# A first stage with no arithmetic on GpSimd, side work paced by time, p and v panels in turn, and nine seven-product panels

## The chip, the cores and the metric

The kernel runs on one core of a Trainium2 chip. The metric is the device time of one execution in microseconds. Five engines share the work: TensorE (PE) multiplies, VectorE (DVE) and ScalarE (ACT) do elementwise work, GpSimd (POOL) does some arithmetic and issues the stores, SyncE (SP) issues the loads. Each engine takes its instructions strictly in the order in which the program emits them, as the rows of the trace show them; semaphores order the engines among each other.

## The reference, cut to what matters

One decoder layer for 1024 prompt tokens and 64 sample tokens (T = 1088 in all), width 1024:

```
mod = silu(c) @ w_mod + b_mod;  shift, scale, gate = split(mod, 3)
h = rmsnorm(x, norm_g) * (1 + scale) + shift
mg, u, va, za, q, k, vb, ob, zb, ig, fg, p, zc = split(h @ w_in)
ya = gelu(u) * spatial_gate(layernorm(gelu(va))) * silu(za)
yb = head_layernorm(sigmoid(ob) * mlstm(q, k, vb, ig, fg, state)) * silu(zb)
yc = (multiscale_pool(p) @ w_pool) * pool_scale * silu(zc)
merged = sum over the three branches of sigmoid(mg) * (y @ w_br)
y = rmsnorm(x + gate * (merged @ w_out))
```

`c` and so `scale` and `shift` differ between the prompt (one row) and the eight sample groups. New states of the mLSTM and of the pooling are outputs too.

## The kernel before, in words

**Products.** Every large product is made in fp32 accuracy from three reduced products: each operand is split into a high part (a cast on ACT) and a low part (a subtraction on DVE, `split`, L205), and PE adds high*high, high*low and low*high. The weights come in panels of 256 columns, each as four raw pieces of 128x512. The class `Stream` loads the pieces (`load`, SP), splits them (`step`: `whi` on ACT at L132, `wlo` on DVE at L101) and keeps at most eight split units.

**Panels.** `b_panel` (L258) makes features x tokens in six units of 24 matmuls of 362 to 364 columns. `a_panel` (L296) makes tokens x features in nine tiles. `seven` (L334) makes a b-panel's result by a seven-product scheme over halves of the inner dimension, of the tokens and of the features: 168 matmuls of 272 columns. It needs summed weights (DVE sums in `step`) and summed activations (`gen_factors`, L757, and `put_t4`, L794). The panels of `SEVEN` are made so: k, zb, zc, u, za and the first MG7 panels of mg; the other mg panels are b-panels in `merge_gates` (L1280).

**Stages.** `start` (L466) makes h and the panels q0 to q3; `seven_panels` (L799) follows; then `inputs_of_mixers` (L910) with `pool_branch` (L1183: p0, va0, p1, va1, ... and `gen_pool`), the panels v0 to v3 and ob0 to ob3; `merge_gates`; `finish` (L1718: the three branch products, then the output product).

**The first stage.** The order of the work is written out by hand in two strings, `PLAN_0` and `PLAN_1` (L1853). Each letter emits one small group of instructions on its engines, and no engine passes over an earlier letter. The letters: `1` loads a panel of w_mod (1 MB), `2` a tile of x (128 features x 1088 tokens, 0.56 MB), `3` a raw piece of w_in; `S` splits half a panel of w_mod; `M` multiplies it with silu(c) (16 matmuls); `C` copies the result out on ACT; `T` turns it on PE and makes two of the eight factors `am` = norm_g*(1+scale) (the first four panels) or shifts `sm` (the last four) on DVE; `Q` squares a tile of x on ACT and adds it to the sum `acc` on POOL (L581); `A`/`V` scale a tile by `am` on ACT or DVE; `H` makes its high part on ACT (L595), `L` its low part on DVE (L601); `W` splits one weight unit; `P`/`R` multiply a tile of x with panel q0 (first eight) or q1 (last eight), high and low parts; `e` makes the reciprocal roots (with a power on POOL); `f` spreads them over the tokens as `rb`; `v`/`g` multiply a tile by `rb` on DVE or POOL (L648); `m` adds the shift and splits the tile into `hhi`, `hlo` (ACT L656, DVE L658); `r` copies q0's or q1's sums out of PSUM; `z`, `s`, `t` make the share of the shift in q0 and q1; `w` keeps PE warm. So q0 and q1 are made from x times `am` before h is known, and `finish_rows` (L703) multiplies their rows by `rb` (on POOL) and adds the shift's share. All these tiles lie in 34 buffers (`slots`).

**After it.** q2 is a b-panel in the usual order, q3 one with all six units open at once (`kouter`), so that `put_t4` may write into h while q3 runs: the product with feature block k done, its factor may be made.

**Side work.** Python generators emit the rest of the work in small steps between the units and tiles of the panels. `tick` (L225) adds to `owed` and takes one step of the first generator per whole unit owed; `pace` sets what a unit or tile adds: 8.5 x pace per a-panel, 6 x pace per b-panel. pace is 1.2 in the pooling stage, 1.5 in v and ob, 1.4 later. The order of the generators: `gen_pool` behind each p panel; behind v0 `gen_gates` (gates of the mLSTM), `gen_sgu` (the spatial gate, three steps per tile of 128 tokens; its mixing product is L1029), `gen_gate` (the layer's gate), `gen_sample` and `gen_prompt` (the mLSTM). A `drain` in `finish` (branch 0, panel 3) ends what is left.

Of the kernel before, what the change touches and what calls it, by code (L numbers as in the profile page):

```python
# [11 lines left out]
ALU = mybir.AluOpType  # L12
# [20 lines left out]
MG7 = 5  # L33
PACE = 1.5
# [124 lines left out]
class Builder:  # L159
# [98 lines left out]
    def b_panel(self, panel, acts, evac, nk=KT, kouter=False, hook=None):  # L258
# [3 lines left out]
        units = [(f, g) for f in range(2) for g in range(3)]  # L262
# [22 lines left out]
        for u, (f, g) in enumerate(units):  # L285
# [7 lines left out]
            self.tick(self.pace / 2)  # L293
        self.st.used(panel)

    def a_panel(self, panel, acts, stack, evac, cols=256, order=range(9)):  # L296
# [4 lines left out]
        for u, t in enumerate(order):  # L301
            p = self.ps()
            if t < 8:
                ts = slice(t * 128, t * 128 + 128)
                for k in range(KT):
# [4 lines left out]
                    if k == 3:  # L310
                        self.tick(self.pace / 2)
# [11 lines left out]
            self.tick(self.pace / 2)  # L323
# [90 lines left out]
    def body(self):  # L414
# [7 lines left out]
        for nm_, ns in [(x, (n,)) for n in range(4) for x in ("p", "va")] + [(x, range(4)) for x in ("v", "ob")]:  # L422
# [43 lines left out]
    def start(self):  # L466
# [52 lines left out]
        A.copy(self.scs[:, :, 0:9], sc)  # L519
        V.tensor_tensor(out=self.scs[:, :, 32:41], in0=sc, in1=self.scs[:, :, 0:9].bitcast(F32), op=ALU.subtract)  # L520
# [9 lines left out]
        def mod_split():  # L530
            n, j = divmod(nxt("ms"), 2)
            raw = raws[n][j]
            hi = self.slot([128, 4, 256], F32R, name="ssh")
            lo = self.slot([128, 4, 256], F32R, name="ssl")
            m = 4 if n else 2
            for q in range(0, 4, m):
                self.split(*(x[:, q : q + m] for x in (raw, hi, lo)))
# [4 lines left out]
        def mod_mul():  # L542
# [3 lines left out]
            for kk in range(KT):  # L546
                for j in range(2):
                    PE.matmul(p[:64, :256], self.scs[:, kk, :], w[kk // 4][j][:, kk % 4, :],
                              start=(kk == 0 and j == 0), stop=(kk == KT - 1 and j == 1))
# [7 lines left out]
        def mod_turn():  # L557
# [3 lines left out]
            if n == 0:  # L561
                V.tensor_scalar(bmod[:, 1, :], bmod[:, 1, :], 1.0, None, ALU.add)
            for j in range(2):
                PE.matmul(p[:, j * 16 : j * 16 + 9], t[:, j * 128 : j * 128 + 128], sel, start=True, stop=True)
# [8 lines left out]
        def square():  # L573
# [4 lines left out]
            else:  # L578
                sq = self.slot([128, T], name="sq")
                A.activation(sq, xs[k], AF.Square)  # L580
                G.tensor_tensor(out=acc[0], in0=acc[0], in1=sq, op=ALU.add)  # L581

        def x_scale(on_act):
            k = nxt("xa")
            x = xs[k]
            V.tensor_tensor(out=bview(x[:, smp]), in0=bview(x[:, smp]), in1=bcol(am[:, k, 1:9]), op=ALU.mult)
            if on_act:
                A.activation(x[:, :TP], x[:, :TP], AF.Copy, scale=am[:, k, 0:1])
            else:
                V.tensor_scalar(x[:, :TP], x[:, :TP], am[:, k, 0:1], None, ALU.mult)  # L590

        def x_high():
            k = nxt("xh")
            hi = self.slot([128, T], F32R, name="xhi")
            A.copy(hi, xs[k])  # L595
# [1369 lines left out]
```

## Time and profile before

| what | value |
|---|---|
| runs, us | 1859.59, 1855.35, 1856.58 (median 1856.58) |
| the profiled execution, its own time | 1857.86 us |
| its span, first to last instruction | 1856.1 us |
| mean granted TensorE clock | 0.985 |
| first stage, to q2's first matmul | 119.31 us |
| q2 and q3 | 57.6 us |
| 25 seven-product panels | from 176.87 to 708.2 us |
| busy over the span: PE, DVE, ACT, POOL | 97%, 58%, 32%, 14% |

The span is the time from the first instruction to the last in the trace; 1.76 us of the execution's own time lie around it. A busy PE in these views is not a PE at its peak, since matmuls overlap; whether a stage runs at its best is seen by comparing its time with that of an undisturbed panel of the same kind.

### The profile page before, as it was taken

The page shows a single profiled execution, that of the slowest core. Times are in us where ns is not written, and L with a number is a line of the kernel's source. Part 1 is how long each engine was busy: PE and PEld are TensorE (multiplying, and loading weights), DVE is VectorE, ACT ScalarE, POOL GpSimd, SP SyncE. Part 2 cuts the span into 40 slices and gives each one's busy share as a digit, 9 for nine tenths or more (in the row PEclk, how much of TensorE's full clock was granted, in tenths as well). Part 3 has the DMA queues.
Part 4 walks back from the last instruction along what each step waited for, and adds up shares of the span by engine and source line. Part 5 has one row for each costly group of instructions (what it writes and reads, how often), then busy time and mean ns, then how long its engine had stood idle before and what let it go on. Part 6 is the DMA issues. An engine that isn't in the chain of part 4 may idle for free.

```text
span 1856.1 us, 32242 instructions
## 1 busy us (share of the span) xinstructions
PE 1796.1 (97%) x13017; PEld 1777.4 (96%) x13017; DVE 1071.9 (58%) x2003; ACT 586.0 (32%) x1141; POOL 262.3 (14%) x427
## 2 busy tenths in 40 slices
PE   7888999999999999999999999999999999999998
PEld 7888999999999998999999899999999999999998
DVE  7777556665666542434527955664655766564444
ACT  5443333333333332222223125332333231131224
POOL 3440000000000001110011212321101101200023
PEclk8988999999999999999999999999999999999999
DMA  6332323332222334333335754776457577694422
GB/s 252 108 128 74 106 94 94 104 122 80 71 70 76 130 106 150 121 123 101 94 116 189 217 180 125 240 237 201 143 175 231 179 228 208 184 317 142 151 62 97
DMA packets 142152, 270.42 MB, mean 146 GB/s; under 512 B 19377, under 2 KB 66161, under 8 KB 142003
## 3 DMA queue, kind: packets, MB, share of 16 engines
q1 hardware_dynamic: 118786, 184.20, 31.4%
q0 software_dynamic: 23072, 83.91, 13.3%
q8 instruction: 102, 1.67, 0.4%
q14 instruction: 48, 0.39, 0.1%
q10 hardware_dynamic: 144, 0.26, 0.0%
HBM read 179.96 MB, written 88.35 MB: 145 GB/s over the span
## 4 chain that ended last, share of the span: by engine, by line
PE 86%; DVE 8%; issue 2%; DMA 2%; ACT 1%; POOL 1%; SPq 0%; POOLq 0%; DVEq 0%; ACTq 0%
PE ps L270 30%; PE ps L308 15%; PE p L362 8%; PE y L362 8%; PE z L362 8%; PE x L362 4%; PE ps L614 2%; PE ps L316 1%; PE ps L1466 1%; PE ps L1264 1%; PE ps L1485 1%; PE ps L1682 1%; PE ps L1439 1%; PE ps L1468 1%; DMA ss<-in_w_mod_dram 1%
## 5 line engine op out<-in xcount | busy, mean ns | idle before, releaser
L101 DVE TENSOR_TENSOR wlo<-raw,whi 128x512 fp32r<-128x512 f32 (+1 forms) x272 | 189.7, 698 | 115.6 <-ACT whi L132 115.6
L308 PE MATMUL ps<-whi,hhi 128*128 128x256 f32 (+1 forms) x768 | 218.5, 284 | 0.0
L308 PE MATMUL ps<-wlo,hhi 128*128 128x256 f32 (+1 forms) x768 | 216.0, 281 | 0.0
L308 PE MATMUL ps<-whi,hlo 128*128 128x256 f32 (+1 forms) x768 | 215.1, 280 | 0.0
L270 PE MATMUL ps<-hhi,whi 128*128 128x362 f32 (+1 forms) x624 | 208.2, 334 | 5.5 <-DVE C L1494 3.4
L270 PE MATMUL ps<-hlo,whi 128*128 128x362 f32 (+1 forms) x624 | 207.0, 332 | 1.9 <-DMA hlo<-b12d 1.7
L270 PE MATMUL ps<-hhi,wlo 128*128 128x362 f32 (+1 forms) x624 | 206.6, 331 | 0.0
L270 PE MATMUL ps<-yhi,whi 128*128 128x362 f32 (+1 forms) x576 | 190.1, 330 | 3.0 <-DVE mgr L1742 1.6
L270 PE MATMUL ps<-yhi,wlo 128*128 128x362 f32 (+1 forms) x576 | 188.7, 328 | 0.0
L270 PE MATMUL ps<-ylo,whi 128*128 128x362 f32 (+1 forms) x576 | 188.5, 327 | 0.0
L132 ACT CAST whi<-raw 128x512 fp32r<-128x512 f32 (+1 forms) x272 | 162.3, 617 | 44.9 <-DVE raw L123 36.3
L308 PEld LDWEIGHTS ps<-whi,hhi 128*128 128x128 f32 x768 | 144.6, 188 | 0.8 <-issue 0.4
L308 PEld LDWEIGHTS ps<-wlo,hhi 128*128 128x128 f32 x768 | 144.7, 188 | 0.0
L308 PEld LDWEIGHTS ps<-whi,hlo 128*128 128x128 f32 x768 | 144.4, 188 | 0.0
L270 PEld LDWEIGHTS ps<-hhi,whi 128*128 128x128 f32 x624 | 119.2, 191 | 6.7 <-DVE C L1494 3.6
L362 PE MATMUL p<-hhi,whi 128*128 128x272 f32 x400 | 116.1, 290 | 7.3 <-ACT row L859 7.3
L270 PEld LDWEIGHTS ps<-hlo,whi 128*128 128x128 f32 x624 | 119.5, 191 | 2.6 <-DMA hlo<-b12d 2.6
L270 PEld LDWEIGHTS ps<-hhi,wlo 128*128 128x128 f32 x624 | 119.4, 191 | 0.0
L362 PE MATMUL p<-hlo,whi 128*128 128x272 f32 x400 | 116.5, 291 | 0.0
L362 PE MATMUL p<-hhi,wlo 128*128 128x272 f32 x400 | 116.3, 291 | 0.0
L132 ACT CAST whi<-sum 128x512 fp32r<-128x512 f32 x75 | 46.6, 621 | 219.7 <-DVE sum L119 144.0
L270 PEld LDWEIGHTS ps<-yhi,whi 128*128 128x128 f32 x576 | 108.2, 188 | 3.7 <-DVE mgr L1742 1.8
(434 smaller groups left out, 4489.6 us busy)
## 6 DMA issues: line engine op xcount, KB each, us to landing
raw<-in_w_in_dram SPq DMA_DIRECT2D x204, 256.0 KB
mgr<-mgd SPq DMA_DIRECT2D x24, 544.0 KB
raw<-in_w_br_dram SPq DMA_DIRECT2D x48, 256.0 KB
out_dram<-C POOLq DMA_DIRECT2D x36, 256.0 KB, 4.5
ylo<-yd SPq DMA_DIRECT2D x16, 544.0 KB
merd<-mgr POOLq DMA_DIRECT2D x16, 544.0 KB, 6.1
C<-in_state_C_dram SPq DMA_DIRECT2D x32, 256.0 KB
mgd<-mg POOLq DMA_DIRECT2D x14, 544.0 KB, 4.6
```

The source lines that it names most:

```text
L101: self.kb.V.tensor_tensor(out=lo, in0=src, in1=hi.bitcast(F32), op=ALU.subtract)
L132: kb.A.copy(hi, src)
L270: self.PE.matmul(ps[:, :n], part(panel, w, k, fs), a[:, g0 : g0 + n], start=(k == 0 and j == 0), stop=(k == nk - 1 and j == 2))
L308: self.PE.matmul(p[:, :cols], a[:, ts], part(panel, w, k, cs), start=(k == 0 and j == 0), stop=(k == KT - 1 and j == 2))
L316: self.PE.matmul(p[:, :cols], stack[:, k, :], part(panel, j, k, cs), start=(k == 0 and j == 0), stop=(k == KT - 1 and j == 1))
L362: PE.matmul(bank[n][:, g, :HT], w[:, ks], b[:, gs], start=(n in (1, 5, 6, 7) and j == 0 and m == 0), stop=(j == 3 and m == 2), skip_group_ ...
L614: PE.matmul(sums[-1][u][:, :m], self.st.part(w, 1 - ww, k, fs), a[:, g0 : g0 + m], start=(k == 0 and part == "high" and j == 0), stop=(k = ...
L1264: self.PE.matmul(p[:, :n], wsl[:, ww, k, fs], a[:, g0 : g0 + n], start=(k == 0 and j == 0), stop=(k == 1 and j == 2))
L1439: PE.matmul(x["ps"][:, h * 128 : h * 128 + 128], k[:, 2 * h + d, :], q[:, 2 * h + d, :], start=(d == 0), stop=(d == 1))
L1466: PE.matmul(p[:, :258], x["qw"][:, 2 * h + d, :], C[x["hp"]][:, h, d, :], start=(d == 0), stop=False)
L1468: PE.matmul(p[:, :258], x["P"][:, a, h, :], x["vs"][:, b, h, :], start=(x["c"] == 0 and j == 0), stop=(j == 2))
L1485: PE.matmul(p[:, :258], x["ks"][:, a, h, d * 128 : d * 128 + 128], x["vs"][:, b, h, :], start=(j == 0), stop=(j == 2))
```

## The change

The first stage takes its arithmetic off POOL (the power in `e` stays) and gets a new plan. The sum of squares is added on DVE. Scaling by `am` is part of `H` (ACT) and of `L` (DVE), so x stays unscaled; `v` applies `am` and `rb` in one DVE instruction; `m` writes h back into the tile of x (`A.activation` into x), and then splits it. q0's rows are multiplied by `rb` on DVE in the side work, q1's as they leave PSUM. The tiles hold h afterwards, so `gen_factors` needs no sums of `hhi` and `hlo`. q3 becomes an ordinary b-panel with the units in the order of tokens from the back (`order`), and a `hook` after each unit calls `drain` and `put_t4`. Four more mg panels go through `seven`. p panels alternate with v panels, va follows; `gen_gates` starts after v0, `gen_sample` and `gen_sgu` with va0, `gen_sample_out` (the end of the old `gen_sample`) and `gen_prompt` after ob3, `gen_gate` in branch 1. `tick` weighs steps, lets no more than 2 be owed, and adds 17/3 x pace per a-panel.

```diff
-MG7 = 5
-PACE = 1.5
+MG7 = 9
+PACE = 1.55
...
+    WEIGHT = dict(gen_pool=0.65, gen_gates=0.65, gen_sgu=0.9, gen_sample_out=0.6, gen_gate=0.7)
...
-        self.owed += n
-        while self.owed >= 1:
-            self.owed -= 1
+        self.owed = min(self.owed + n, 2.0)
+        while self.side:
+            w = self.WEIGHT.get(self.side[0].__name__, 1.0)
+            if self.owed < w:
+                break
+            self.owed -= w
             self.advance(self.side)
...
                     if k == 3:
-                        self.tick(self.pace / 2)
+                        self.tick(self.pace / 3)
...
-        for nm_, ns in [(x, (n,)) for n in range(4) for x in ("p", "va")] + [(x, range(4)) for x in ("v", "ob")]:
+        for nm_, ns in [(x, (n,)) for n in range(4) for x in ("p", "v")] + [(x, range(4)) for x in ("va", "ob")]:
...
-                G.tensor_tensor(out=acc[0], in0=acc[0], in1=sq, op=ALU.add)
+                V.tensor_tensor(out=acc[0], in0=acc[0], in1=sq, op=ALU.add)
...
         def x_high():
             k = nxt("xh")
+            x = xs[k]
             hi = self.slot([128, T], F32R, name="xhi")
-            A.copy(hi, xs[k])
+            A.activation(hi[:, :TP], x[:, :TP], AF.Copy, scale=am[:, k, 0:1])
+            V.tensor_tensor(out=bview(x[:, smp]), in0=bview(x[:, smp]), in1=bcol(am[:, k, 1:9]), op=ALU.mult)
+            A.copy(hi[:, smp], x[:, smp])
...
         def x_low():
...
-            V.tensor_tensor(out=lo, in0=xs[k], in1=xsp[k][0].bitcast(F32), op=ALU.subtract)
...
+            V.scalar_tensor_tensor(out=lo[:, :TP], in0=x[:, :TP], scalar=am[:, k, 0:1], in1=hi[:, :TP].bitcast(F32),
+                                   op0=ALU.mult, op1=ALU.subtract)
+            V.tensor_tensor(out=lo[:, smp], in0=x[:, smp], in1=hi[:, smp].bitcast(F32), op=ALU.subtract)
...
-        def h_scale(eng):
-            x = xs[nxt("hs")]
-            eng.tensor_tensor(out=x, in0=x, in1=rb[0], op=ALU.mult)
+        def h_scale():
+            k = nxt("hs")
+            x = xs[k]
+            V.scalar_tensor_tensor(out=x[:, :TP], in0=x[:, :TP], scalar=am[:, k, 0:1], in1=rb[0][:, :TP], op0=ALU.mult,
+                                   op1=ALU.mult)
+            V.tensor_tensor(out=x[:, smp], in0=x[:, smp], in1=rb[0][:, smp], op=ALU.mult)
+            V.tensor_tensor(out=bview(x[:, smp]), in0=bview(x[:, smp]), in1=bcol(sm[:, k, 1:9]), op=ALU.add)
...
-            A.activation(hh[:, :TP], x[:, :TP], AF.Identity, bias=sm[:, k, 0:1])
-            A.copy(hh[:, smp], x[:, smp])
-            V.scalar_tensor_tensor(out=hl[:, :TP], in0=x[:, :TP], scalar=sm[:, k, 0:1], in1=hh[:, :TP].bitcast(F32),
-                                   op0=ALU.add, op1=ALU.subtract)
-            V.tensor_tensor(out=hl[:, smp], in0=x[:, smp], in1=hh[:, smp].bitcast(F32), op=ALU.subtract)
+            A.activation(x[:, :TP], x[:, :TP], AF.Identity, bias=sm[:, k, 0:1])
+            self.split(x, hh, hl)
...
         def finish_rows(n):
-            for f in range(2):
-                G.tensor_tensor(out=rows[n][f], in0=rows[n][f], in1=rb[0], op=ALU.mult)
+            shift_turn()
             yield
             for f in range(2):
                 r = rows[n][f]
+                if n == 0:
+                    V.tensor_tensor(out=r, in0=r, in1=rb[0], op=ALU.mult)
...
+        def hook(u):
+            if u == 2:
+                self.drain()
+            if u > 3:
+                for j in range(2):
+                    self.put_t4(2 * u - 8 + j)
...
-        self.b_panel(self.pan["q", 3], self.h, self.evac_rows(3, self.qd), kouter=True, hook=hook)
-        self.drain()
+        self.b_panel(self.pan["q", 3], self.h, self.evac_rows(3, self.qd), hook=hook, order=(2, 1, 0, 5, 4, 3))
...
-            t = self.slot([128, T], name="fac")
-            V.tensor_tensor(out=t, in0=hh.bitcast(F32), in1=hl.bitcast(F32), op=ALU.add)
...
+        a, b = self.xs.pop(j), self.xs.pop(j + 4)
...
+        self.side += [self.gen_sample(), self.gen_sgu()]
         for n in range(4):
-            self.a_panel(self.pan["v", n], self.h, self.hs, self.evac_tok(n, self.vd, "copy"),
-                         cols=264 if n == 0 else 256)
-            if n == 0:
-                self.side += [self.gen_gates(), self.gen_sgu(), self.gen_gate(), self.gen_sample(), self.gen_prompt()]
+            self.a_panel(self.pan["va", n], self.h, self.hs, self.evac_tok(n, self.vad, "gelu"))
...
 Builder.PLAN_0 = (
-    "wSS3w21M2W2CT1QVwSH4SL2wPQMV2Q1CWTHR21VSPHLSPMQ3Q2RVHLRLCTPVWSRHL23SPWQQMC3RVTHAHLLwPRQV3H"
-    "LPSSRPR1WS3"
+    "1223w 1223wQQSSwMCTHHWLLw SSMC1223QQTPHHWPLLRR SSMC1223QQTPHHWPLLRR SSMC13QQTPHHWPLLRR 13WPPRRe"
 )
 Builder.PLAN_1 = (
-    "rW13SeSM1CPP3MS3PCfRTSgMCgPWSvRgTMgCRTvRTPzmWRmsmgPmPWmWgPRRmtms3R3WmW3tr"
+    "r3WPR 1SSMCPRffTvm 1SSMCPRWvmPRT SSMC3vmPRWvmPRT SSMC3vmPRvmPRTzs 3vm3vmsWWWWr"
 )
```

More of the change, by code (lines that the diff above doesn't have):

```diff
@@ L255, in prep_some, with b_panel @@
                 self.st.step()
-    def b_panel(self, panel, acts, evac, nk=KT, kouter=False, hook=None):
+    def b_panel(self, panel, acts, evac, nk=KT, kouter=False, hook=None, order=(0, 1, 2, 3, 4, 5)):
         self.st.need(panel)
         part = self.st.part
-        units = [(f, g) for f in range(2) for g in range(3)]
+        units = [divmod(u, 3) for u in order]
         def mms(ps, f, g, k):
@@ L482, in mod_load @@
             raws[n] = [self.slot([128, 4, 256], name="ss") for _ in range(2)]
-            m = 4 if n else 2
-            for j in range(0, KT, m):
-                S.dma_start(raws[n][j // 4][:, j % 4 : j % 4 + m], i["w_mod"][panels[n]][:, j : j + m, :])
+            for j in range(2):
+                S.dma_start(raws[n][j], i["w_mod"][panels[n]][:, 4 * j : 4 * j + 4, :])
         def x_load():
@@ L531, in mod_split @@
             n, j = divmod(nxt("ms"), 2)
[L532 removed]
             hi = self.slot([128, 4, 256], F32R, name="ssh")
             lo = self.slot([128, 4, 256], F32R, name="ssl")
[L535 to L537 removed]
+            self.split(raws[n][j], hi, lo)
             wsp.setdefault(n, []).append((hi, lo))
@@ L547, in mod_mul @@
                 for j in range(2):
-                    PE.matmul(p[:64, :256], self.scs[:, kk, :], w[kk // 4][j][:, kk % 4, :],
-                              start=(kk == 0 and j == 0), stop=(kk == KT - 1 and j == 1))
+                    PE.matmul(p[:64, :256], scs[:, kk, :], w[kk // 4][j][:, kk % 4, :], start=(kk == 0 and j == 0),
+                              stop=(kk == KT - 1 and j == 1))
         def mod_copy():
@@ L631, in rms_sum @@
             self.rsqrt(rs, ms, rt)
-            acc.clear()
+            rb.append(self.slot([128, T], name="rb"))
         def rms_rows():
-            rb.append(self.slot([128, T], name="rb"))
-            for b in range(3):
-                p = self.ps()
-                n = 0
-                for t in range(4 * b, min(9, 4 * b + 4)):
-                    m = 128 if t < 8 else 64
-                    PE.matmul(p[:, n : n + m], rs[:m, t : t + 1].to_broadcast([m, 128]), self.ident[:m, :m],
-                              start=True, stop=True)
-                    n += m
-                A.copy(rb[0][:, b * 512 : b * 512 + n], p[:, :n])
@@ L646, in h_scale @@
-        def h_scale(eng):
-            x = xs[nxt("hs")]
-            eng.tensor_tensor(out=x, in0=x, in1=rb[0], op=ALU.mult)
+            b = nxt("rr")
+            t0, t1 = ((0, 4), (4, 9))[b]
+            ps = [self.ps() for _ in range(-(-(t1 - t0) // 4))]
+            for t in range(t0, t1):
+                m = 128 if t < 8 else 64
+                o = (t - t0) % 4 * 128
+                PE.matmul(ps[(t - t0) // 4][:, o : o + m], rs[:m, t : t + 1].to_broadcast([m, 128]), self.ident[:m, :m],
+                          start=True, stop=True)
@@ L882, in load @@
             return w
+        scs = self.slot([128, KT, 64], F32R, name="scs")
+        V.tensor_copy(scs, self.zero.unsqueeze(1).to_broadcast([128, KT, 64]))
+        self.A.copy(scs[:, :, 0:9], self.sc)
+        V.tensor_tensor(out=scs[:, :, 32:41], in0=self.sc, in1=scs[:, :, 0:9].bitcast(F32), op=ALU.subtract)
         nxt = load(0)
@@ L1763, in finish @@
                     self.side2.append(self.prep_y(1))
+                if n == 0 and xi == 2:
+                    self.side.append(self.gen_gate())
                 if n < 3 or xi == 2:
```

147 lines of the change are left out of this document (69 added, 78 removed).

## The prediction, made before the changed kernel was run

> **What bounds the kernel now.** I read the page, then busy time by stretches cut at the matmuls that open and close a stage, then who waited for whom.
>
> ```profile
> PE 1796.1 (97%) x13017; PEld 1777.4 (96%) x13017; DVE 1071.9 (58%) x2003; ACT 586.0 (32%) x1141; POOL 262.3 (14%) x427
> ```
>
> PE is the engine to beat, but 97% hides where it runs slowly. The stretches below are: the first stage in two halves; q2; q3; the first seven-product panel; the second; the two panels ob0 and ob1 with the spatial gate beside them; a quiet b-panel; a quiet a-panel. The columns are length, then busy time (and count) of each engine, granted clock, DMA share, GB/s.
>
> ```profile
> core 0: us, PE busy (x) PEld busy (x) DVE busy (x) ACT busy (x) POOL busy (x), PEclk, DMA share, GB/s
> 0.94:60.16 59.22, 47.81 (x304) 44.28 (x305) 46.52 (x52) 34.53 (x42) 20.41 (x8) 0.88 0.61 220
> 60.16:119.31 59.15, 47.25 (x301) 45.02 (x301) 45.75 (x57) 22.64 (x40) 29.05 (x17) 0.90 0.34 114
> 119.31:145.60 26.29, 26.29 (x146) 26.29 (x146) 16.91 (x26) 12.62 (x21) 7.79 (x7) 0.90 0.45 156
> 145.60:176.87 31.27, 24.00 (x146) 23.70 (x145) 27.72 (x35) 12.15 (x21) 1.06 (x2) 0.93 0.08 28
> 176.87:200.65 23.78, 23.78 (x169) 23.78 (x170) 9.87 (x15) 7.11 (x12) 1.06 (x2) 0.88 0.27 94
> 200.65:221.72 21.07, 21.07 (x171) 21.07 (x170) 10.59 (x16) 7.23 (x12) 1.06 (x2) 1.00 0.31 107
> 1011.70:1088.00 76.30, 68.59 (x563) 67.03 (x561) 67.86 (x119) 11.38 (x28) 19.53 (x24) 0.98 0.67 204
> 1725.10:1749.00 23.90, 23.90 (x146) 23.90 (x146) 12.87 (x22) 5.67 (x10) 0.00 (x0) 1.00 0.10 32
> 1749.00:1773.50 24.50, 24.50 (x210) 24.50 (x209) 11.22 (x23) 9.07 (x37) 5.34 (x8) 1.00 0.89 293
> ```
>
> A b-panel costs 23.90 us at full clock, a seven-product panel 21.07, an a-panel 24.50. Three places are above that: the first stage (24 us of PE idle, clock 0.88 to 0.90), q2 to the first seven-product panel, and the stretch of the spatial gate. The waits of PE up to 200 us and in the later stretch:
>
> ```profile
> PE ps L688 <- ACT smp L681: 8.0, 1, 8.0
> PE p L362 <- ACT row L859: 7.3, 1, 7.3
> ```
>
> ```profile
> PE ps L1029 <- DVE va L1019: 4.9, 4, 1.5
> ```
>
> The first of these is not ACT's doing. ACT stood behind DVE, and DVE behind POOL, as the order in time shows (start, length):
>
> ```profile
> 105.57 0.68 DVE L101 TENSOR_TENSOR wlo<-raw,whi 128x512 fp32r<-128x512 f32 x1
> 106.17 7.97 DVE L653 TENSOR_TENSOR x<-x,sm 128x64 f32<-128x64 f32 x1
> 114.07 1.27 DVE L658 SCALAR_TENSOR_TENSOR hlo<-x,sm,hhi 128x1024 fp32r<-128x1024 f32 x1
> 115.26 0.21 DVE L660 TENSOR_TENSOR hlo<-x,hhi 128x64 fp32r<-128x64 f32 x1
> ```
>
> ```profile
> 106.64 2.53 POOL L648 TENSOR_TENSOR x<-x,rb 128x1088 f32<-128x1088 f32 x1
> 109.13 4.92 POOL L705 TENSOR_TENSOR row<-row,rb 128x1088 f32<-128x1088 f32 x2
> ```
>
> A 64-element instruction of 0.21 us took 7.97 us: it ended when POOL's three products did. POOL arithmetic is paid for on DVE.
>
> **First stage, prices.** Groups of DVE and POOL, then of ACT, up to q3's end (after the bar: busy us, mean ns):
>
> ```profile
> L658 DVE SCALAR_TENSOR_TENSOR hlo<-x,sm,hhi 128x1024 fp32r<-128x1024 f32 x8 | 10.2, 1278 | 4.4 <-ACT hhi L656 4.3
> L765 DVE TENSOR_TENSOR fac<-hhi,hlo 128x1088 f32<-128x1088 f32 x8 | 10.0, 1282 | 0.0
> ```
>
> ```profile
> L581 POOL TENSOR_TENSOR acc<-acc,sq 128x1088 f32<-128x1088 f32 x7 | 20.4, 2913 | 33.8 <-ACT sq L580 33.5
> L217 POOL TENSOR_TENSOR rs<-ms,mhalf 128x9 f32<-128x9 f32 x1 | 1.8, 1819 | 11.7 <-DVE ms L630 11.7
> ```
>
> ```profile
> L207 ACT CAST ssh<-ss 128x1024 fp32r<-128x1024 f32 x14 | 14.6, 1049 | 4.9 <-PE ps L614 3.0 <-DVE ssl L208 1.1 <-DMA ss<-in_w_mod_dram 0.8
> L132 ACT CAST whi<-raw 128x512 fp32r<-128x512 f32 x18 | 11.0, 618 | 3.4 <-DVE raw L123 2.3 <-DMA raw<-in_w_in_dram 1.1
> L656 ACT ACTIVATE hhi<-x,sm 128x1024 fp32r<-128x1024 f32 x8 | 9.2, 1147 | 0.0
> L595 ACT CAST xhi<-x 128x1088 fp32r<-128x1088 f32 x8 | 8.8, 1098 | 12.8 <-DVE x L590 12.8
> L580 ACT ACTIVATE sq<-x 128x1088 f32<-128x1088 f32 x7 | 7.6, 1106 | 1.6 <-DMA x<-in_xT_dram 1.6
> L554 ACT COPY smp<-ps 64x256 f32<-64x256 f32 x8 | 2.9, 364 | 12.8 <-PE ps L548 12.7
> L657 ACT CAST hhi<-x 128x64 fp32r<-128x64 f32 x8 | 1.9, 240 | 11.8 <-DVE x L653 11.8
> ```
>
> So a wide two-input DVE instruction is 1.28 us, a small one 0.21, and a wide ACT pass 1.05 to 1.15. PE's letters stand one behind the other here: P from 43.21, M from 45.19, R from 47.02, T from 48.10; so P 1.98, M 1.83, R 1.08, T 0.6. The pair of `am` takes DVE 0.48.
>
> ```profile
> 43.21 0.33 PE L614 MATMUL ps<-xhi,whi 128*128 128x364 f32 x1
> ...
> 45.19 0.28 PE L548 MATMUL ps<-ssh,scs 128*64 128x256 f32 x1
> ...
> 47.02 1.15 PE L614 MATMUL ps<-xlo,whi 128*128 128x364 f32 x6
> 48.10 0.61 PE L564 MATMUL ps<-c_sel,smp 64*128 64x9 f32 x4
> ```
>
> ```profile
> 10.64 0.48 DVE L569 TENSOR_SCALAR am<-ps,c_bmodT,c_norm_gT 128x9 f32<-128x9 f32 x2 [0.29 <-PE ps L564]
> ```
>
> **First stage, the new plan.** In sums it looks lighter. But a section `SSMC..QQTPHHWPLLRR` is a chain through queues that keep their order. DVE has S S, the two additions of Q Q, T's `am`, the small products of H H, W, L L, and then the next section's S S. From the second S of one section to that of the next: half of M 0.9, C 0.37; Q Q on ACT 2.2 (behind C there) and the last addition 1.28; `am` 0.48 (T has long run, but `am` stands behind the additions); H H 2 x (1.15+0.24); W 0.62 on ACT and 0.68 on DVE; L L 2 x 1.49; S S 2.56. That is 14.9 us; neighbours in a queue overlap by about 0.07 us each (114.07+1.27 against 115.26), so I take 14.4. PE has 1.83+0.6+2x1.98+2x1.08 = 8.6 us of work in it and idles for the rest. Before, POOL took the additions and the order was interleaved, and `e` began at 60.16, where the table's first row ends.
>
> Head: Q Q waits for x1, behind 2.1 MB at the 405 GB/s of the opening (row below, 3 us a slice; 5.2 us from about 3 us on, landing near 9.5); Q Q, S S, M, C, T, H H, W, L L then end near 24 us. Three sections: 67. R 1.1, then `e` from 68, about 2 us: 70. The power 1.82 with its small DVE instructions, then `r` and W: 75.5.
>
> ```profile
> GB/s 56 289 223 344 413 411 406 404 407 408 397 131 0 0 8 0 14 161 66 197 0 131 304 283 356 70 0 87 5 0 0 93 321 61 170 127 146 0 0 93
> ```
>
> PLAN_1: S S 2.5, M, C, P R (3.1), f f, T, `sm` 0.4: the first `v` at 84.5. A `vm` is serial too: v on DVE 1.28+0.21+0.21, two ACT passes 1.15+1.10, the subtraction 1.28: 5.1 us with overlaps, in which DVE waits 2.3, for nothing behind the subtraction may pass it. Eight: 41. Between them DVE has S S three times (7.5), W twice and q2's first (2.0), three T (1.3), z (1.1): 53 in all. q2's first matmul is at 137.5 us, 18 later than the 119.3 of before, with nothing gone wrong.
>
> Two things come on top. Clock: before, q2 took 26.29 instead of 23.90 us behind the 8.0 us wait, so an idle stretch costs up to 2.4 us. The new stage has some eight stretches of 5 us and more; M and T, and in PLAN_1 the P and R ahead of T, lie on the chain. Between 0 and 8 x 2.4 = 19 I take 11. The Trainium skill ("TensorE: Matmul & The Clock Gate", section "Why this matters for your kernels") warns of gaps over about 3 us between bursts, behind which the clock is halved for at least a window of 3.4 us; an estimate from that page, half of 3.4 us for eight gaps, is 14 us, and the sum would be 3 higher. Buffers: in PLAN_1 eight x, fourteen to sixteen parts, scs, rb, two rows and six raw halves of w_mod leave hardly a pair of the 34 free, and S's parts wait for R; 0 to 6, I take 3. q2 starts at 152 (138 to 162): **+32 us** (+18 to +43).
>
> **q2, q3 and the first seven-product panel** take 26.29+31.27+23.78 = 81.3 us against 2 x 23.90+21.07 = 68.9. The 7.3 us wait for ACT's copies was that of six units closing together; now one copy is left (0.5), and no halved clock behind it. `put_t4` touches h's upper tokens only once u4 is through, and u5 reads the lower ones. The factors lose eight additions (10.0 us), POOL two products. q2 still starts at a halved clock (2.4) and takes in the two T of the shift (1.2): **-7.5** (-10 to -4).
>
> **Four more seven-product panels:** 4 x (23.90-21.07) = **-11.3**. DVE's 10.59 of 21.07 us leaves room.
>
> **Spatial gate.** PE idles 7.7 us of 76.3, clock 0.98: 9.2 us at most. DVE has 67.86 for 25.5 steps (17 half-ticks of 0.75 per panel), less 8 splits of 0.68: 2.45 per step. New: 17 x 1.55/3/0.9 = 9.8 steps, 24+2.7 = 26.7 us of DVE per panel; PE 24.50+0.77 x (34.3-24.5) = 32. DVE stops being the bound: **-8.5** (-10 to -5).
>
> **Pooling.** Steps come at 0.65, 13.5 per panel in place of 10.2, up to three at once. `gen_pool`'s matmuls stand seven steps in and so about 4 us earlier, while the DVE chain ahead of them stays; they waited 0.3 us before:
>
> ```profile
> PE ps L1264 <- DVE plo L208: 0.3, 1, 0.3
> ```
>
> Up to 4 us for each of the two widest windows: **+3** (0 to +8). The rest (prompt steps 9.3 per b-panel in place of 8.4, `gen_gate` in branch 1, where DVE has 12.87 of 23.90): **+1** (-2 to +5). The loads and stores of moved steps go with them, on SP and POOL; the DMA share in the table (0.10 in branch 1, 0.67 in the densest) and the raw pieces loaded ahead cover them, and I cost them at nothing; without that cover a load that a step waits for would hold DVE's queue, not PE's, for some us, which the +5 holds.
>
> Sum: 1857.86+32-7.5-11.3-8.5+3+1 = 1866.6 on the scale of the profiled execution's 1857.86; that one was 1.3 above the median of the runs, so I say 1865.
>
> **The rivals.** *POOL was the bound.* DVE's demand, 92.3 busy before, falls to 86 (47 wide at 1.28: Q 7, L, v and h's split 8 each, S 16; 12 W at 0.68; 32 small at 0.21; 8 T at 0.48; some 7 for the rest), and the stage follows it: 119.3 x 86/92.3 = 111, so -8 in place of +32: 1825. The 7.97 us speaks for it, DVE's in-order chain against it. It decides where q2's first matmul comes before 142.6, since the other terms sum to -23.3. The Trainium skill ("GPSIMD Engine Reference", section "3. Performance versus the Vector engine") would have it so, with about 1 cycle an element on Vector and 2.6 on GpSimd; the rows agree on such a price (1.28 against 2.91 us), but a price says nothing of the order. Chance 0.15. *The chain holds, but clock and buffers cost nothing:* q2 at 138, 1865-14 = 1851; for it, PE's slack in each section; against it the clock column. Chance 0.18. *The side work is late as well:* the pooling waits at +8, the prompt at +5 and q2 at 162: 1865+5+4+10 = 1884. Chance 0.07. My forecast has 0.60.
>
> **The numbers.** About 0.2% (3.7 us) is what a measurement tells from no change. Forecast and third rival are slower, but for the forecast's lowest tenth (0.06), which is within; the second rival is half within, half below (0.09 each); the first is faster: faster 0.24, same 0.15, slower 0.61. The range goes from 1843, which takes in the second rival with other terms at their good ends, to 1881, with the clock and the buffers near theirs; the first rival is left out below and the third above. The forecast's own range is 1854 to 1881.
>
> **What would show it.** In the profile after: q2's first matmul (L270's successor, hhi) near 152; DVE waiting for ACT ahead of `hl` some 2.3 us eight times; no POOL TENSOR_TENSOR but the power; wide DVE instructions at 1.28; no wait of 7 us ahead of the first `p<-hhi,whi`; 29 seven-product panels of 21.1; the mixing's wait under 2 us. q2 before 142.6, or a pooling stage with waits over 8 us, would make the forecast wrong.

## The result, and the profile after

The changed kernel takes 1890.30 us (median of 4 runs, 1889.79 to 1890.61) against 1856.04 for the kernel before (4 runs, 1855.35 to 1859.59): 1.018 times as long, 95% interval 1.0163 to 1.0198, 34 us slower. The prediction said 9 us slower, 1843 to 1881: the side is right, the size is not, and the time lies above the range. The profiled execution took 1890.37 us, its span is 1887.9, its mean granted clock 0.973.

The page of the changed kernel, from its first part and its slices:

```profile
PE 1798.9 (95%) x13105; PEld 1775.5 (94%) x13105; DVE 1079.7 (57%) x2062; ACT 607.0 (32%) x1156; POOL 213.3 (11%) x410
...
PE   5868999999999999999999997998999999999998
...
PEclk7888999999999999999999998999999999999999
```

Total work is as before (PE 1796.1 then). The first three slices are thinner (5, 8, 6 tenths), and there are new dips around slices 25 and 28. Busy time by stretches, cut at the matmuls that open a stage: the first stage at the same two places as in the prediction (q2 began at 119.31 then), the rest of the first stage, q2, q3, the first seven-product panel; then va1, va2, va3, mg9, and panel 0 of branch 1:

```profile
0.94:60.16 59.22, 35.79 (x214) 33.01 (x215) 28.82 (x45) 25.48 (x35) 0.02 (x1) 0.76 0.51 188
60.16:119.31 59.15, 48.53 (x266) 45.35 (x265) 25.70 (x45) 23.35 (x33) 4.25 (x5) 0.80 0.34 113
119.31:151.60 32.29, 19.56 (x113) 18.46 (x111) 18.90 (x30) 15.12 (x19) 2.16 (x4) 0.84 0.12 43
151.60:178.80 27.20, 27.04 (x152) 26.06 (x153) 18.20 (x32) 11.68 (x18) 2.67 (x5) 0.94 0.50 171
178.80:203.40 24.60, 24.06 (x146) 23.76 (x144) 17.98 (x25) 11.08 (x20) 1.06 (x2) 1.00 0.20 68
203.40:224.70 21.30, 21.29 (x169) 21.29 (x170) 11.23 (x17) 8.16 (x14) 1.06 (x2) 1.00 0.22 66
```

```profile
1076.40:1109.20 32.80, 31.25 (x265) 31.08 (x264) 17.43 (x42) 9.98 (x21) 8.60 (x22) 1.00 0.58 187
1109.20:1146.40 37.20, 33.17 (x264) 32.60 (x264) 19.80 (x48) 12.64 (x29) 9.33 (x23) 0.95 0.52 172
1146.40:1187.60 41.20, 34.35 (x264) 33.78 (x263) 19.26 (x47) 11.10 (x25) 11.79 (x29) 0.88 0.56 186
1306.90:1345.60 38.70, 31.80 (x197) 31.06 (x195) 18.44 (x62) 10.52 (x24) 5.39 (x11) 0.91 0.72 214
1670.70:1707.20 36.50, 32.36 (x193) 30.18 (x193) 28.71 (x42) 12.76 (x18) 1.72 (x2) 0.95 0.82 283
```

q2 begins at 151.6 us, 32.3 later. q2 to the first seven-product panel take 73.1 us, 8.2 less. The 28 further seven-product panels end at 816.6: four more cost 84.4 us, where four b-panels cost 95.6. So at the end of the seven-product panels the change stands 12.9 us behind, as forecast (+13.2). The other 19 us are lost later, where -4.5 was forecast. There the engines wait for one another: in va3 PE is busy 34 of 41 us, DVE 19, ACT 11. The waits of PE from p0 to mg11, first three rows:

```profile
PE ps L1675 <- DVE qz L1639: 10.7, 3, 6.4
PE ps L1370 <- DVE t L1358: 6.5, 1, 6.5
PE ps L275 <- DMA hlo<-b12d: 1.9, 3, 1.2
```

The sample tokens' products (L1675, beside va1 to va3) and the transposes of their output (L1370, in mg9) are the new waits; the clock falls behind both (0.95, 0.88, 0.91). To share out the 19 us, I took each panel's length less the sum of its matmuls at the median spacing of their kind, in both traces; the figures move by about 1 us with how finely the kinds are told apart. The excess is: beside va0 to va3 18.9 (where the sample work ran before, it was 2.1), mg9 8.8 (0.4), panel 0 of branch 1 7.2 (nothing); and to the good, the panels beside the spatial gate's mixing 1.6 where it had been 11.1, and mg11, which had waited 3.4 us for a state update, nothing where it had been 5.2. What is left of the 19 us, 1.3, I put down to pooling.

In the first stage, DVE's two largest waits:

```profile
DVE acc L583 <- ACT sq L582: 20.0, 4, 8.7
DVE hlo L208 <- ACT hhi L207: 18.9, 8, 4.0
```

Eight waits ahead of `hlo`, 2.36 us each: the prediction had 2.3. But look at the engine sums as well: no engine is near full, and DVE is busy 73.4 of 150.7 us.

### The profile page after: what moved, and what is told of

It reads as the page before. It is cut to its first block, busy times and chain, and to the rows that moved or that the text cites. A ratio compares the mean times of both kernels' runs of the same rounds, so it can differ in the third digit from the quotient of the medians.

```text
span 1887.9 us, 32483 instructions
## 1 busy us (share of the span) xinstructions
PE 1798.9 (95%) x13105; PEld 1775.5 (94%) x13105; DVE 1079.7 (57%) x2062; ACT 607.0 (32%) x1156; POOL 213.3 (11%) x410
## 5 line engine op out<-in xcount | busy, mean ns | idle before, releaser
L101 DVE TENSOR_TENSOR wlo<-raw,whi 128x512 fp32r<-128x512 f32 x272 | 187.6, 692 | 65.5 <-ACT whi L132 65.4
L132 ACT CAST whi<-raw 128x512 fp32r<-128x512 f32 x272 | 162.2, 617 | 41.0 <-DVE raw L123 39.6
L275 PE MATMUL ps<-hhi,whi 128*128 128x362 f32 (+1 forms) x432 | 145.4, 337 | 7.0 <-ACT whi L132 5.6
L275 PE MATMUL ps<-hlo,whi 128*128 128x362 f32 (+1 forms) x432 | 144.1, 334 | 2.1 <-DMA hlo<-b12d 1.9
L275 PE MATMUL ps<-hhi,wlo 128*128 128x362 f32 (+1 forms) x432 | 143.8, 333 | 0.2 <-DVE wlo L101 0.2
L369 PE MATMUL p<-hhi,whi 128*128 128x272 f32 x464 | 133.3, 287 | 0.6 <-ACT row L852 0.6
L369 PE MATMUL p<-hlo,whi 128*128 128x272 f32 x464 | 133.8, 288 | 0.0
L275 PEld LDWEIGHTS ps<-ylo,whi 128*128 128x128 f32 x576 | 108.8, 189 | 3.8 <-DVE ylo L208 3.8
L275 PEld LDWEIGHTS ps<-yhi,wlo 128*128 128x128 f32 x576 | 108.8, 189 | 0.4 <-DVE wlo L101 0.4
L275 PEld LDWEIGHTS ps<-hhi,whi 128*128 128x128 f32 x432 | 83.0, 192 | 8.5 <-ACT whi L132 5.9
```

The source lines that it names most:

```text
L101: self.kb.V.tensor_tensor(out=lo, in0=src, in1=hi.bitcast(F32), op=ALU.subtract)
L132: kb.A.copy(hi, src)
L275: self.PE.matmul(ps[:, :n], part(panel, w, k, fs), a[:, g0 : g0 + n], start=(k == 0 and j == 0), stop=(k == nk - 1 and j == 2))
L369: PE.matmul(bank[n][:, g, :HT], w[:, ks], b[:, gs], start=(n in (1, 5, 6, 7) and j == 0 and m == 0), stop=(j == 3 and m == 2), skip_group_ ...
```

## The experiments

All times are medians of 4 runs, beside 7 runs of the kernel before on the same chip (medians 1856.0 to 1857.3); the ratio's 95% interval stands in brackets. "q2 at" is the start of q2's first matmul in the profile. The first stage and q2 are the same code in the changed kernel and in *m_head*, *m_out* and *m_gate* below, and yet q2 starts at 149.8 to 153.0 us in their profiles and q3 at 178.8 to 183.0; a difference of that size between two kernels shows no effect of an edit.

### Which half of the change loses what

*first_alone* takes the hunks of `start`, `gen_factors`, `b_panel`, `evac_rows` and the plans; *side_alone* all the others, with `MG7 = 5`.

> Before with the new first stage alone (its plans, q3's order of units, the factors made from the tiles of x); five seven-product mg panels, old paces, old order of panels and of side work. Theory A, the terms of the prediction: the first stage costs 32 us and q2 to the first seven-product panel gives 8 back, nothing behind that moves: 1856 + 24 = 1880 us, q2's first matmul near 151. Theory B, the waits in the later stages of the changed kernel come from what the new first stage leaves behind (buffers, the order of queues): 1856 + 24 + 19 = 1899.

> Before with the new side work alone (pace and weights, p and v in turn, order of the generators, the gate in branch 1), old first stage, five seven-product mg panels. Theory A, the side work itself loses the time (the sample work beside va, its output right behind ob3, the gate in branch 1): 1856 + 19 = 1875 us with waits for qz of some 10 us, for t ahead of the transposes of 6 us and for wgs and ylo in branch 1. Theory C, the new order is sound and only the four missing b-panels of mg leave it too little room: 1856 - 8 = 1848 and none of these waits over 3 us.

first_alone: 1886.25 us (1.0136 to 1.0172), q2 at 152.9. In its profile the span is 28.2 us longer: 33.6 in the first stage, 5.3 given back up to the first seven-product panel; from there on no stage (p0 to ob3, mg, the branches, the output) differs by more than 0.3 us from the kernel before. The time is 6 above theory A and 13 below theory B, and the profile has none of B's waits; the 6 are partly q2, which took 30.1 us here. side_alone: 1870.93 us (1.0057 to 1.0093), span 13.6 longer, with 8.3 us of waits for qz and Cs and 6.6 for t; va2, va3 and the panel behind ob3 take 37 to 40 us. So theory C is out: the waits come with the new side work, with five seven-product panels too. Branch 1 waits 0.7 us here, not 7: that part of theory A is missed, and needs both halves or the nine panels. The halves add: 28.2 + 13.6 - 11.3 = 30.5 of 31.8 us.

### The first stage: POOL, order, clock

Only POOL is taken out, in the old plan:

```diff
-                G.tensor_tensor(out=acc[0], in0=acc[0], in1=sq, op=ALU.add)
+                V.tensor_tensor(out=acc[0], in0=acc[0], in1=sq, op=ALU.add)
...
-            "g": lambda: h_scale(G)
+            "g": lambda: h_scale(V)
...
-                G.tensor_tensor(out=rows[n][f], in0=rows[n][f], in1=rb[0], op=ALU.mult)
+                V.tensor_tensor(out=rows[n][f], in0=rows[n][f], in1=rb[0], op=ALU.mult)
```

> The kernel before, with its plan and all else as it was, but the additions of squares, the g products and the rows' products of the first stage on DVE instead of POOL. Theory A, the new stage is slow by its order and not by the move from POOL to DVE: DVE takes 17 wide instructions of 1.28 us, 22 us, and is rid of the 12 to 15 us in which POOL kept it out, so q2 starts within 6 us of 119.3 and the time lies between 1850 and 1864. Theory H, the move itself is the price: q2 20 us later or more, over 1875.

no_pool: 1838.35 us (0.9883 to 0.9916), q2 at 99.3. Neither theory: 20 us *earlier*. DVE's groups up to q2, first in the kernel before, then here (busy, mean ns):

```profile
L601 DVE TENSOR_TENSOR xlo<-x,xhi 128x1088 fp32r<-128x1088 f32 x8 | 12.5, 1569 | 1.7 <-ACT xhi L595 1.7
...
L590 DVE TENSOR_SCALAR x<-x,am 128x1024 f32<-128x1024 f32 x7 | 9.8, 1395 | 0.0
L653 DVE TENSOR_TENSOR x<-x,sm 128x64 f32<-128x64 f32 x7 | 9.3, 1324 | 0.0
```

```profile
L601 DVE TENSOR_TENSOR xlo<-x,xhi 128x1088 fp32r<-128x1088 f32 x8 | 10.3, 1288 | 2.1 <-ACT xhi L595 2.1
...
L590 DVE TENSOR_SCALAR x<-x,am 128x1024 f32<-128x1024 f32 x7 | 5.2, 748 | 0.0
```

```profile
0.94:99.30 98.36, 91.64 (x604) 86.48 (x604) 76.37 (x120) 56.80 (x81) 6.43 (x10) 0.93 0.56 201
```

DVE does more here (13 of the wide instructions fall in the stage, 16.7 us at 1.28) and is busy 76.4 us instead of 92.3: POOL's 49 us of work (20.41 and 29.05 in the prediction's rows) had cost DVE some 33 (92.3 + 16.7 - 76.4). The one-input scaling L590, too, took longer beside POOL, but not evenly. Its shortest, median and longest, in the kernel before and here:

```profile
L590 DVE TENSOR_SCALAR x<-x,am x7: 739/746/3026, 12.0 to 55.1; 128x1024 f32<-128x1024 f32 x7
```

```profile
L590 DVE TENSOR_SCALAR x<-x,am x7: 745/748/751, 12.4 to 50.3; 128x1024 f32<-128x1024 f32 x7
```

Two of the seven took 3.0 us, for 2.95 of which an addition on POOL was running, and the other five the 0.74 us that they take without POOL; the mean of L653 is that of one instruction of 7.97 us and six of 0.21. In these rows an instruction was held or not at all. The Trainium skill ("SBUF — State Buffer", section "Terms") calls the port pair of the two engines lock-allocated and exclusive, "held for the full instruction"; these rows agree.

So the move off POOL is worth 20 us, and what came with it costs 52. *old_order* keeps all the new instructions and puts the letters in the old order:

```diff
 PLAN_0
-1223w 1223wQQSSwMCTHHWLLw SSMC1223QQTPHHWPLLRR SSMC1223QQTPHHWPLLRR SSMC13QQTPHHWPLLRR 13WPPRRe
+1wSS3w21M2W2CT1QwSHSL2wPQM2Q1CWTHR21SPHLSPMQ3Q2RHLRLCTPWSRHL23SPWQQMC3RTHHLLwPRQ3HLPSSRPR1WS3
 PLAN_1
-r3WPR 1SSMCPRffTvm 1SSMCPRWvmPRT SSMC3vmPRWvmPRT SSMC3vmPRvmPRTzs 3vm3vmsWWWWr
+rW13SeSM1CPP3MS3PCffRTSvMCvPWSvRvTMvCRTvRTPzmWRmsmvPmPWmWvPRRmms3R3WmW3r
```

> The changed kernel with its new letters put in the order of the old plans (A, V and t fall away, g becomes v, f stands twice, the shift of the sample tokens stands in m instead of v). The move from POOL to DVE alone, in the old order, brought q2's first matmul to 99.3 us, the changed kernel has it at 151.6. Theory A, the order of the plans is what costs: q2 between 99 and 112, 1890 - 45 = 1845 us. Theory B, the new letters cost (one more pass of ACT per tile, x kept in its buffers): q2 over 135, 1873 or more.

old_order: 1843.93 us (0.9915 to 0.9944), q2 at 96.7. Theory A. Only the order of the letters (with one `3` and one `w` more, and one small addition moved from `v` to `m`) lies between this and 1890.30. PE is now busy for 88.5 of the stage's 95.8 us and keeps its clock:

```profile
0.94:96.70 95.76, 88.53 (x597) 84.00 (x598) 66.64 (x110) 55.91 (x77) 6.01 (x10) 0.95 0.55 196
```

q2 behind it takes 37.9 us instead of 27, with PE waiting 4.7 us ahead of the shift's turn: 11 of the 55 us are given back.

Two repairs inside the new plan ask which link of the chain counts. *f_am* moves the next section's S S ahead of H, M C behind H, and the loads one section up (`SSMC..QQTPHHWPLLRR` becomes `..QQT SSPHHMC1WPLLRR`); *f_h* puts S between v and m and M behind the pair (`vSmvSmMC3PRWPRT`); *f_t* then puts M ahead of the m's and T ahead of P R (`vSvSMC3mmTPRWPR`).

> The changed kernel with another order in the first plan: the splits of the next w_mod panel stand ahead of H, its M and C behind H, so that M runs beside L and T waits for the additions alone; each w_mod panel is loaded one section earlier. Theory A, the chain S, M, C, Q, T, H, L sets a section's 15.3 us: a section takes 11 to 12, q2 starts 7 to 11 us earlier, 1881 us. Theory G, DMA, DVE's demand or the clock sets it: the sections stay at 15 us, within 4 us of 1890.

> The changed kernel with another order in the second plan: each v is followed by one S (or W) ahead of its m, and M stands behind the pair; the same instructions on the same engines. Theory A, the chain in DVE's queue sets the stage and DVE's eight waits of 2.3 us for ACT ahead of hlo are part of it: they shrink to 1 us and under, q2 starts 10 to 16 us earlier, 1877 us. Theory G, the demand of the engines or PE's slow clock sets it: q2 stays within 4 us of 151.6, 1888 to 1892.

> The changed kernel with a third order in the second plan: v S v S, then M and C, then m m, then T, and the two P R behind T. In the order tried before, DVE's waits for ACT ahead of hlo fell from 18.9 to 6.4 us and its waits for T's products rose from 8.2 to 25.3, for T stood behind two P R. Theory A, the loop from S over M, C and T to the next v sets the stage: both waits fall under 8 us, a pair of tiles takes 10 to 11 us in place of 13 to 14, q2 starts 8 to 14 us earlier, 1879 us. Theory G, the engines' demand or the slow clock sets it: within 4 us of 1890.

f_am: 1882.04 us (1.0124 to 1.0154), q2 at 142.0, 9.6 earlier; from one `am` to the next, a section takes 11.0 and 11.3 us (`am` at 34.84, 45.88 and 57.19): theory A. f_h: 1896.18 us (1.0198 to 1.0229), q2 at 149.5 and q2 itself 5.5 us longer: a miss. DVE's waits from 70 to 152 us show where it went:

```profile
DVE sm L573 <- PE ps L566: 25.3, 4, 7.2
DVE hlo L208 <- ACT hhi L207: 6.4, 7, 1.5
```

The waits for ACT went (18.9 to 6.4), but T now stood behind two P R on PE's queue, and DVE waited for `sm` instead (8.2 before). f_t: 1884.66 us (1.0132 to 1.0162), q2 at 140.7, 11 earlier, of which q2 gives 5.5 back. The same waits there, up to 152 us:

```profile
DVE hlo L208 <- ACT hhi L207: 17.3, 8, 4.4
...
DVE sm L573 <- PE ps L566: 7.2, 1, 7.2
```

Theory A is missed here too: the waits for `hlo` are nearly as long as in the changed kernel, and a pair of tiles takes 13.5 to 14.2 us (the first `v` of each pair at 94.06, 108.29, 121.78 and 135.56) instead of 10 to 11 (14.1 and 13.3 in the changed kernel). q2's start misleads in these two orders. A `W` stands ahead of the last tiles in them, so that q2 starts before the last tile of h is made and no longer has this wait of the changed kernel ahead of it:

```profile
PE ps L275 <- ACT whi L132: 5.6, 1, 5.6
```

The last `hlo` ends at 152.0 us in the changed kernel (150.2 to 153.5 in the others of the same code), at 148.3 in f_t and at 157.1 in f_h. So neither order made the loop shorter; the wait moved along it, and f_t's 5.6 us of time go with the earlier `W` and the somewhat earlier last tile. DVE's wait for ACT, on which I had built the term, is not by itself the link that counts: in f_h it shrank by 12.5 us and nothing was gained. That the order as a whole is the cause, old_order shows, where letters of other panels stand in between; which link of the second plan's loop sets its time stays open.

The clock. 18 small products of zeros ahead of each M but the first, ahead of the first s and of q2:

```diff
- SSMC
+ SSxMC
...
+"x": lambda: keep_warm(18)
```

> The changed kernel with 18 small products of zeros ahead of each M but the first, of the first s and of q2, where PE stood idle for 2.5 to 5.7 us: PE keeps its clock, nothing else moves. Theory J, the term of the prediction: the slow clock is worth 11 us of the first stage, so q2 starts 7 to 11 us earlier, 1881 us. Theory K, the products at half clock mostly lie beside waits for DVE and the order alone is worth the 32 us: q2 moves by 3 us at most, 1887 to 1891, though the granted clock of the stage rises from 0.80 to over 0.90.

warm: 1891.00 us (1.0170 to 1.0200), q2 at 150.5. The same stretch in the changed kernel, then in this one:

```profile
0.94:152.00 151.06, 104.28 (x589) 97.22 (x590) 73.83 (x120) 64.36 (x87) 6.43 (x10) 0.80 0.36 127
```

```profile
0.94:152.00 151.06, 120.58 (x915) 112.01 (x916) 74.91 (x121) 65.42 (x88) 6.43 (x10) 0.86 0.36 127
```

The clock rose from 0.80 to 0.86 (not over 0.90), q2 came 1.1 us earlier and the time did not move, as theory K has it. Its reason does not hold, though. From the third `am` to the fourth, in the changed kernel and in this one:

```profile
50.34:65.74 15.40, 10.59 (x49) 9.66 (x48) 8.87 (x15) 7.26 (x10) 0.00 (x0) 0.69 0.25 79
```

```profile
49.25:63.34 14.09, 11.45 (x94) 10.43 (x93) 8.87 (x14) 7.27 (x10) 0.00 (x0) 1.00 0.29 100
```

DVE and ACT do the same work, and with M's products at 0.28 us instead of 0.41 the section is 1.3 us shorter; the one before it took 14.16 instead of 15.23. In m_out, whose code is the same up to q2, the fourth M ran fast without any added product, and that section took 14.10. So the slow clock lies on the chain, at 1.1 to 1.3 us a section, and `e` began 3.2 us earlier in warm (73.4 for 76.6). The added products took it back: the next 18 hold PE from 81.52 to 84.82, while the first operands of the M behind them are ready, and that M begins at 84.75, as in the changed kernel (84.57). The M after it (from 97.7) stayed slow. What the clock is worth over the whole stage, this run can't say.

### The side work: three places

*m_head*:

```diff
+            if bb == 7:
+                kms.pop(h)
+                head(h + 1)
             parts(x + 2)
...
             if bb == 7:
-                kms.pop(h)
-                head(h + 1)
                 finish_head(h)
```

> The changed kernel, with the preparation of the next head (qz, km) emitted ahead of the split of the next state tile instead of behind it. Theory A, the waits of PE for qz come from DVE's queue, where the split that waits for a late load of C stands ahead of qz: the 10.7 us wait falls under 2, and the time by 8 to 12: 1880 us. Theory D, the loads of C are late altogether: PE then waits for Cs instead and the time stays within 3 us of 1890.

DVE in va3 of the changed kernel, in order of time, shows what it mends:

```profile
1170.27 0.68 DVE L101 TENSOR_TENSOR wlo<-raw,whi 128x512 fp32r<-128x512 f32 x1
1174.82 0.70 DVE L208 TENSOR_TENSOR Cs<-C,Cs 128x516 fp32r<-128x516 f32 x1 [3.86 <-ACT Cs L207]
1175.43 0.87 DVE L1685 SCALAR_TENSOR_TENSOR C<-C,decb,ps 128x258 f32<-128x258 f32 x2
1176.22 0.49 DVE L1639 CAST qz<-qh 128x64 fp32r<-128x64 f32 x4
```

DVE waits 3.9 us for the high part of a state tile two steps ahead (ACT in turn waits for a buffer that a store still reads); qz, which PE needs now and which has long been possible, stands behind. m_head: 1884.60 us (1.0129 to 1.0166). In the profile the wait for qz falls to 2.4 us (not under 2), the sixteen panels from p0 to ob3 from 490.3 to 481.7 us:

```profile
PE ps L1370 <- DVE t L1358: 6.4, 1, 6.4
PE ps L275 <- DVE ylo L208: 2.9, 2, 2.3
PE ps L1675 <- DVE qz L1639: 2.4, 3, 1.4
```

Theory A in the stage; the time gained 5.7 of the 8.6, since the first stage and q2, the same code, were 3.8 us longer in that profile.

*m_out* puts `for _ in range(6): yield` behind the load of `o`. DVE's row in mg9 of the changed kernel:

```profile
L1709 DVE SCALAR_TENSOR_TENSOR t<-o,t 64x256 f32<-64x256 f32 x4 | 1.6, 404 | 6.4 <-DMA o<-od 6.4
```

> The changed kernel, with six empty steps between the load of the sample rows of o and the work on them. Theory A, PE's 6.5 us wait ahead of the transposes comes from DVE waiting 6.4 us for that load, which waits for ob3's store: the wait goes and the slow clock behind it, 1890 - 8 = 1882 us. Theory E, the steps put off make the prompt work late and a later wait takes the place: within 3 us of 1890.

m_out: 1884.97 us (1.0130 to 1.0169). The wait is gone, mg9 takes 27.0 us instead of 38.7 and is 8.1 nearer to its work without idle time; new waits in mg10 and mg11 take 4.6 of that, branches 2 and 1 give 3.2: 6.7 us of gain behind the seven-product panels, 5.3 in the time. Theory A, with a part of theory E.

The two mends take back 15.3 of the 32 us lost beside va, in mg9 and in branch 1. Some 8 us beside va, where PE's listed waits are short in m_head, and 7 in branch 1 are left, and what causes them is not shown.

*m_gate*: `if n == 1 and xi == 2` where the change has `n == 0`.

> The changed kernel, with the gate's side work begun one panel later in branch 1 (panel 1 instead of 0). Theory A, the 7.2 us that panel 0 of branch 1 is over its ideal come from the gate's splits and loads standing beside the splits and loads of branch 1's own inputs: 1890 - 6 = 1884 us. Theory F, the loads of branch 1 are late by themselves or the gate costs the same wherever it stands: within 3 us of 1890.

m_gate: 1896.97 us (1.0201 to 1.0232): a miss. Panels 0 to 2 of branch 1 take 87.5 us instead of 86.1. PE's waits there:

```profile
PE ps L893 <- DVE wgs L208: 2.8, 3, 1.6
PE ps L275 <- DVE ylo L208: 2.5, 2, 2.1
```

Panel 0 still waits for branch 1's own input (`ylo`), and the gate's own waits went along to the next panels. The gate is not what makes `ylo` late; that it is the prompt work, which now ends in branch 0 at 1639 us, was not tried. 5 us of the longer time aren't explained by branch 1; 4 of them are the first stage and q2, the same code, again.

### Parts put together

*np_q3* is no_pool with q3 of the change (its unit order, its hook, all factors as side work, still summed from h's parts); *np_q3_mg9* adds `MG7 = 9` to it, with the old side work; *old_mended* is old_order with m_head and m_out; *all_new* is np_q3 with nine panels, the new side work, m_head and m_out.

> The kernel before with the first stage's arithmetic off POOL in the old plan, and q3 as in the change (ordinary panel, units from the back, all factors as side work); the factors are still summed from h's parts. Theory A, q3's 7.3 us wait came from six units that close together: q2 to the first seven-product panel from 78 to 70 us, 1838 - 8 = 1830 us. Theory I, the eight sums of the factors, that the change does without, keep DVE late: 1835 or more.

> The same with nine seven-product mg panels and the old side work. Theory A, four panels at 2.83 us less: 1830 - 11 = 1819 us. Theory C, the old side work needs the four b-panels of mg: the steps left over are emitted at once in branch 0 and PE waits there, 1824 or more.

> The changed kernel with the old order of the first stage (1843.9 us) and both mends of the side work: qz and km ahead of the split of the state, six empty steps ahead of the sample's output. Theory A, the causes are separate and add: 1843.9 - 8.6 - 6.7 = 1829 us. Theory L, they share a wait (one mend only moves what the other leaves): 1834 or more.

> The kernel before with its first stage off POOL, q3's new order, nine seven-product mg panels, and the new side work with both mends. Theory A, the parts add: to the end of the seven-product panels 763 us as with the old side work, then the changed kernel's 1071.3 us less 8.6 and 6.7: span 1819, time 1821 us. Theory C, nine panels leave the side work too little room whatever its order: 1830 or more.

np_q3: 1830.75 us (0.9843 to 0.9872), 7.6 under no_pool: theory A. np_q3_mg9: 1865.98 us (1.0029 to 1.0062), 35 *more*: theory C, and far more of it than its 5 us. Its span reaches 763 us at the end of the seven-product panels, as summed, and then 114 us pass from the first matmul of panel 2 of branch 0 to that of panel 3, 79 of them behind panel 2's last matmul, where the prompt steps left over are emitted at once:

```profile
1511.90:1626.30 114.40, 87.60 (x517) 80.68 (x515) 86.08 (x269) 24.52 (x72) 17.40 (x37) 0.88 0.44 121
```

old_mended: 1829.39 us (0.9831 to 0.9867). all_new: 1821.47 us (0.9794 to 0.9823), q2 at 99.3. Both are within 1 us of what the parts sum to (1828.6 and 1821): the causes are separate as far as the first stage's own variation lets one see. With the new side work the nine panels pay: from p0 to the end the changed kernel takes 1071.3 us, and side_alone, with five, 1162.8 less four b-panels (95.6), so 4 us are lost there for the 11.3 saved. all_new is 34.5 us faster than the kernel before and 69 faster than the changed one. Its page:

```profile
PE 1781.4 (98%) x13113; PEld 1760.8 (97%) x13113; DVE 1092.4 (60%) x2070; ACT 601.5 (33%) x1154; POOL 214.6 (12%) x410
```

## Why the prediction was right and wrong

**First stage, +32: right in sum (32.3; q2 at 151.6 for 152), wrong in its parts.** The chain was the cause: nearly the same letters in another order have q2 at 96.7, and with S S moved ahead of H a section takes 11.0 to 11.3 us. A section took 15.2 to 15.4 us for 14.4 (`am` at 35.11, 50.34 and 65.74), but 14.1 where M ran at full speed; so the summed chain was good to 0.3 us, and the slow clock was there, at 1.1 to 1.3 us a section where the prediction had 1.4 for each of eight gaps. What failed in the sum is what it left out. Ahead of `e` it has one R of 1.1 us where the plan has P P R R (6.1 us by its own prices): `e` came 4.1 us behind the last L. The head took 26.4 us for 24. With these, the sections and 1.4 us more from `e` on, the first `v` came at 94.6 for 84.5; from there to q2 it was 57 us for 53. How much of that 4 us is clock, and what the 3 us for buffers are worth, was not tested. So the sum came out by luck: letters left out took the place of a part of the 14 us for clock and buffers.

**"POOL was the bound" as a rival: the mechanism is shown, the alternative was false.** I held it against the chain as if one of them had to be untrue. Both hold: off POOL the stage gains 20 us (no_pool), and the new order takes 55 (old_order against the changed kernel; 46 in the time). Its time of 111 came from DVE's busy sum less only the contention that I had seen; the stretched L590, L601 and L653 stood in the groups too. In the new stage DVE was busy for 73.4 us, not for the 86 that the rival reckoned with.

**q2 to the first seven-product panel, -7.5: right** (-8.2; np_q3 alone gains 7.6 in the time). **Four seven-product panels, -11.3: right in place** (-11.3), but their price isn't all in that place: with the old side work the four b-panels missing cost 46 us elsewhere.

**Spatial gate, -8.5: right** (-9.5; the mixing waits 0.7 us for 4.9). The panels that the prediction calls ob0 and ob1 are v3 and ob0. **Pooling, +3: right within its range** (+1.3, as what is left over).

**"The rest", +1 (-2 to +5): the step that failed**, with this sentence: "The loads and stores of moved steps go with them ... without that cover a load that a step waits for would hold DVE's queue, not PE's, for some us, which the +5 holds". It measured about +27: the sample work beside va 16.8 more, its output 8.4, branch 1 7.1, less 5.2 for mg11. DVE's queue *is* PE's queue where the next product's small operand stands behind the step that waits (m_head), and a step placed right behind the panel whose store it reads (m_out) held DVE for 6.4 us: POOL issued the store at 1308.67, the load went out behind its landing at 1310.80, and DVE went on at 1314.4. I costed `gen_sgu`, `gen_pool`, the prompt and the gate; `gen_sample` and `gen_sample_out` were moved as well, and I put them at nothing.

## What to carry to other kernels

Where a program emits in order, cost a moved step by the slowest thing that it waits for at its *new* place, a store just issued above all, and then list what is queued behind it on each engine and who needs that next. A hand-written order is part of the kernel: when its letters change, keep the interleaving, and check a term of the sum letter by letter against the plan; here the change with its new letters in the old order is 13 us faster than the kernel before, and in its own tidy order 34 slower. And work taken off the critical engine (four cheaper panels) takes cover from the side work that ran beside it, so the two have to be changed together.

## What the runs showed of the hardware

Arithmetic on POOL beside DVE held not only two-input DVE instructions but a one-input scaling too: two of seven took 3.0 us, the others 0.74, and all seven 0.75 without POOL. The Trainium skill ("GPSIMD Engine Reference", section "1. Specifications") names two kinds that contend, two inputs in SBUF and the modes with two ports; the rows agree on the first, and the mode in which the scaling ran is not in the trace. The size, some 33 us of DVE's time for 49 us of POOL's, is what I had not expected.

The granted clock counts where slow products lie on the chain: a section of the plan took 15.40 us at 0.69 and 14.09 at 1.00, with DVE and ACT busy for the same 8.9 and 7.3 us. Products added to keep it up are no free cure, for they stand in PE's queue themselves (3.3 us ahead of one M), and over the whole stage nothing was gained.
